# A decoder layer in one launch: first loads in smaller pieces from two queues, the first product by column halves, and r turned without copies

## The chip, the cores and the metric

The kernel runs on one core of one Trainium2 chip. The metric is the device time of one execution in microseconds (us), the median of three runs. The engines that matter are TensorE (PE, matrix products; PEld is its weight load), VectorE (DVE), ScalarE (ACT), GpSimd (POOL) and SyncE (SP, which here issues loads and stores). Each engine works through its own list of instructions strictly in that list's order and waits on semaphores where it needs the result of another engine or of a transfer. An instruction on SP or on ScalarE can also issue a transfer (DMA) between the chip's memory (HBM) and the on-chip buffers.

## The reference

One layer (DEPTH is 1) for a sequence of 1024 tokens with 1024 columns, all in 32-bit floats. What matters here:

```python
h = rms_norm(x, norm_mix_g)                 # r = (mean(x*x) + EPS) ** -0.5, a number per token
proj = h @ w_in                             # q, k, v, gates, convolution inputs ...
... gated linear attention, short convolution, merge, output projection ...
x = x + merged @ w_out
ple_gate = sigmoid(rms_norm(x, norm_ple_g) @ w_ple_gate)
x = x + ple_gate * (p @ w_ple_proj)         # p: 1024 x 256, w_ple_proj ("W_pe"): 256 x 1024
return rms_norm(x, norm_final_g)
```

The product `p @ w_ple_proj` depends on nothing else in the layer. The kernel computes it first, while x is still on its way, and keeps it in HBM until the end.

## The kernel before

*How a product is made.* Every 32-bit operand is split into a high part (a rounded copy, cast by ScalarE) and a low part (operand minus high part, by VectorE): `split`, line 594. A product is then three passes on TensorE, high by high, high by low and low by high (`mm3`, line 605). All passes accumulate in one PSUM bank of 128 rows by 512 columns.

*How the order comes about.* The kernel's code does not issue instructions, it notes them (`Flow.note`, line 270) with an estimated cost and latency each. `set_dues` gives every operation a due time, counted back from where TensorE's list of main products needs it. `put_in_order` then builds each engine's list greedily: at every step it takes the engine that can go first, and there, of the operations that are ready by the estimate, the one with the earliest due time. For a load issued by SP it models one shared pipe (`pipe`) for the landing. The field `hurry` moves due times forward. A changed estimate in the first microseconds can therefore change the order of later instructions too.

*The start* (phase `prep0`, from line 938). Nine products of zeros warm TensorE up. SP issues the loads of p (transposed on the host, as two contraction tiles of 128 rows each) and of W_pe (two tiles as well), each in pieces of 128 x 512, that is 256 KB: for the first half of p (`halves[0]`, tokens 0 to 511) and the first half of W_pe's columns first, W_pe and p in turn. The planner sets W_pe's piece first. After them come the second half of W_pe's columns, the x loads (`get_x`, tiles `hq`, 512 KB each), and the second half of p.

`pe_blocks` (line 1007) makes the product in blocks of 128 tokens by 512 columns. The first call takes tokens 0 to 511 (four blocks) and columns 0 to 511 with `by_kt=True`: all four blocks with the first contraction tile, then all four with the second. Each block and tile is one `mm3`, so the first call has 24 products, of which the first twelve need only the first tiles of p and W_pe. Finished blocks are copied out of PSUM by ScalarE and VectorE in turn and stored (`ped`).

*r of the input* (`scale_h`, line 976). ScalarE squares x (`sq`, `sr`), VectorE adds, TensorE sums over rows by products with a column of ones (`ms`), VectorE adds EPS and GpSimd takes the power -0.5 (`r_x`). r then stands with the token on the partition, and is wanted with the token along the columns and equal in all partitions: VectorE copies each of the four columns of r 128 times (`rb`, 128 x 512), TensorE transposes the four 128 x 128 squares (`rt`), and VectorE multiplies x by r and the gain (`hq`). `scale_h` runs twice, once for each half of the tokens.

*After the start* the layer's large products follow, first for the gates (`ga0pX` and so on), then the V stage (`vX`, `vV`, `vY`), into which the decay of the attention is woven: `zp` products, ScalarE's `t`, VectorE's `c` with a scan. From there on to the end TensorE works on products of the same form.

Of the kernel before, what the change touches and what calls it, by code (L numbers as in the profile page):

```python
# [16 lines left out]
P = 128  # L17
# [239 lines left out]
class Flow:  # L257
# [12 lines left out]
    def note(self, engine, op, call, args, kw):  # L270
        views = [a for a in args if isinstance(a, View) or hasattr(a, "ap")]
        views += [a for k, a in kw.items() if k not in ("out", "accum_out") and (isinstance(a, View) or hasattr(a, "ap"))]
        outs, ins = ([kw["out"]], views) if "out" in kw else (views[:1], views[1:])
        if kw.get("accum_out") is not None:
            outs.append(kw["accum_out"])
        o = Op()
        o.n, o.engine, o.call, o.args, o.kw = len(self.ops), engine, call, args, kw
        o.side, o.table, o.bytes, o.bufs, o.hurry = self.side, 0, 0, [], self.hurry
        label = lambda v: v.buf.name if isinstance(v, View) else "in"
        o.name = f"{label(outs[0])}<-{','.join(label(v) for v in ins)}"  # L280
        shape = outs[0].shape
        n = 1
        for d in shape[1:]:
            n *= d
        o.lat = 0.15
        if engine == PE:
            o.cost, o.lat = n / 2400 + 0.0134, 0.22
            if op == "transpose" or args[1].dtype == F32:
                o.cost = 0.11
            elif args[1].shape[0] < P:  # L290
                o.cost = 0.42
        elif engine == DVE:
            psum = any(isinstance(v, View) and v.buf.pool.name == "ps" for v in outs + ins)
            o.cost = 0.07 + n * (0.00055 if op in ("tensor_scalar", "tensor_copy") and not psum else 0.00104)
            if op in ("scalar_tensor_tensor", "tensor_scalar"):
                o.cost += 0.06
            if op == "tensor_tensor_scan":
                o.cost = 0.05 + n * 0.0021
        elif engine == ACT:
            o.cost = 0.10 + n * 0.000833 + (0.1 if "accum_out" in kw else 0.0)  # L300
            o.table = TABLE.get(args[2] if len(args) > 2 else None, 0)
        elif engine == POOL:
            o.cost = 0.1 + n * 0.001 if op == "memset" else 0.6
        else:
            o.cost, o.bytes = 0.4, shape[0] * n * 4
            if getattr(ins[0], "apart", None):
                o.cost, o.bytes = 0.6, 1.4 * o.bytes
            o.lat = 2.0 + o.bytes / 250e3
        preds = {}

        def behind(p):
            if p is not None and p != o.n:
                q = self.ops[p]
                lat = q.lat
                if q.engine == engine and engine != SP:
                    lat = 0.0 if engine == PE else 0.08
                preds[p] = max(preds.get(p, 0.0), lat)

        for v in ins:
            if isinstance(v, View):  # L320
                for b in v.blocks():
                    e = v.buf.memory.setdefault(b, [None, []])
                    behind(e[0])
                    e[1].append(o.n)
        for v in outs:
            if isinstance(v, View):
                for b in v.blocks():
                    e = v.buf.memory.setdefault(b, [None, []])
                    for p in [e[0]] + e[1]:
                        behind(p)  # L330
                    e[0], e[1] = o.n, []
                if engine == PE:
                    behind(v.buf.group)
                    v.buf.group = o.n
                for pool in v.buf.pool.instead:
                    for old in pool.buffers:
                        for p in old.users:
                            behind(p)
        for v in outs + ins:
            if isinstance(v, View) and v.buf not in o.bufs:  # L340
                if v.buf.index is None:
                    v.buf.index = len(v.buf.tag.buffers)
                    v.buf.tag.buffers.append(v.buf)
                o.bufs.append(v.buf)
                v.buf.users.append(o.n)
        o.preds, o.succs = preds, []
        for p in preds:
            self.ops[p].succs.append(o.n)
        self.ops.append(o)
        if self.bundle is not None and engine == PE:  # L350
            self.bundle.append(o)
# [163 lines left out]
def kernel(  # L515
# [83 lines left out]
    def mm(*a, **kw):  # L599
        nc.tensor.matmul(*a, skip_group_check=True, **kw)  # L600

    def transpose(o, i):
        nc.tensor.transpose(o, i, ident)
# [262 lines left out]
    def rows(b):  # L866
        return slice(b * P, (b + 1) * P)
# [70 lines left out]
    with phase("prep0") as pool:  # L938
# [10 lines left out]
        def get_x(i):  # L949
            for n in (0, 3) if i == 0 else (1, 2):  # L950
                for kp in range(0, 4, 2):
                    kk = 4 * quad[n][1] + kp
                    load(q[n][:, kp:kp + 2, :], xT[:, kk:kk + 2, halves[i]])

        nc.hurry = 8.0
        for kt in range(2):
            load(pr_[:, kt, halves[0]], pT[:, kt, halves[0]])
            load(wr_[:, kt, halves[0]], wpe[:, kt, halves[0]])
        for kt in range(2):
            load(wr_[:, kt, halves[1]], wpe[:, kt, halves[1]])  # L960
        nc.hurry = 0.0
        get_x(0)
        load(vec, vecs)
        for kt in range(2):
            load(pr_[:, kt, halves[1]], pT[:, kt, halves[1]])
        get_x(1)
        load(trim, tri)

        def split_half(hi, lo, src, hh):
            nc.hurry = 8.0  # L970
            for kt in range(2):
                cs = halves[hh]
                split(hi[:, kt, cs], lo[:, kt, cs], src[:, kt, cs])
            nc.hurry = 0.0

        def scale_h(i):


            both = (0, 3) if i == 0 else (1, 2)
            acc = slot(1, "hl"[i], f"sq{i}", (4, 512), F32)  # L980
            for j, (n, kp) in enumerate((n, kp) for n in both for kp in (0, 2)):
                d = acc[:, 0:2, :] if j == 0 else acc[:, 2:4, :] if j % 2 else slot(2, "hl"[i], f"sr{i}", (4, 512), F32)[:, 0:2, :]
                act(d, q[n][:, kp:kp + 2, :], AF.Square, scale=1.0 / 32.0)
                if j:
                    tt(acc[:, 0:2, :], acc[:, 0:2, :], d, op=ALU.add)
            sums = pso.tile([P, 4, P], F32, tag="o", name=f"ms{i}", bufs=2)
            for s in range(4):
                for kt in range(2):
                    mm(sums[:, s, 0:1], acc[:, kt, s * P:(s + 1) * P], ones, start=kt == 0, stop=kt == 1)
            r = sm.tile([P, 4], F32, tag="rx", name=f"r_x{i}", bufs=2)  # L990
            nc.vector.tensor_scalar(r, sums[:, :, 0], EPS, None, op0=ALU.add)
            nc.gpsimd.tensor_tensor(r, r, mhalf[:, 0:1].to_broadcast([P, 4]), op=ALU.pow)
            rb = bp.tile([P, 4, P], F32, tag="u2", name=f"rb{i}", bufs=2)
            nc.vector.tensor_copy(rb, r[:, :, None].to_broadcast([P, 4, P]))
            rt = pso.tile([P, 4, P], F32, tag="o", name=f"rt{i}", bufs=2)
            for s in range(4):
                transpose(rt[:, s, :], rb[:, s, :])
            rt = rt.rearrange("p s t -> p (s t)")
            for n in both:
                for k in range(4):  # L1000
                    kk = 4 * quad[n][1] + k
                    stt(q[n][:, k, :], q[n][:, k, :], gmix[:, kk:kk + 1], rt, op0=ALU.mult, op1=ALU.mult)
# [4 lines left out]
        def pe_blocks(bs, c, by_kt=False):  # L1007
# [5 lines left out]
            todo = [(b, kt) for kt in range(2) for b in bs] if by_kt else [(b, kt) for b in bs for kt in range(2)]  # L1013
            for b, kt in todo:
                nc.side = at[0] > len(BANKS)
                mm3(acc[b - bs[0]], pth[:, kt, rows(b)], ptl[:, kt, rows(b)], wph[:, kt, halves[c]],
                    wpl[:, kt, halves[c]], kt == 0, kt == 1)
                nc.side = True
                if kt == 1:
                    t = bp.tile([P, 512], F32, tag="T", name=f"pe{b}_{c}", bufs=4)  # L1020
                    (nc.vector.tensor_copy if b % 2 else nc.scalar.copy)(t, acc[b - bs[0]])
                    store(ped[b][:, halves[c]], t)
# [16 lines left out]
                c.cons(0, 0, X)  # L1039

        nc.hurry = 8.0
        for kt in range(2):
            split(pth[:, kt, halves[0]], ptl[:, kt, halves[0]], pr_[:, kt, halves[0]])
            split(wph[:, kt, halves[0]], wpl[:, kt, halves[0]], wr_[:, kt, halves[0]])
        nc.hurry = 0.0
        pe_blocks(range(0, 4), 0, True)
        split_half(wph, wpl, wr_, 1)
        pe_blocks(range(0, 4), 1)
        split_half(pth, ptl, pr_, 1)
        pe_blocks(range(4, 8), 0)  # L1050
        pe_blocks(range(4, 8), 1)
        scale_h(0)
# [747 lines left out]
```

## Time and profile before

| what | value |
|---|---|
| median of 3 runs | 1086.59 us (1086.43 to 1086.79) |
| the profiled execution, its own time | 1086.71 us |
| its span, first to last instruction | 1084.8 us |
| TensorE busy | 1071.5 us, 99% of the span |
| VectorE busy | 870.0 us, 80% |
| ScalarE busy | 598.9 us, 55% |
| GpSimd busy | 49.3 us, 5% |
| transfers | 237.85 MB, 219 GB/s in the mean |
| granted TensorE clock | 0.997 |

The span leaves out some 1.9 us of the execution that lie around it. Times in the profile's rows count from the span's start. A row of the timeline has the start, the length, the engine, the source line, the operation and "out <- in" by the program's tile names; nearly all operations carry line 503, where the planned order is issued, so they are told apart by tile names. In brackets stands how long the engine was idle before it and what it waited for. "SPq" is the issue of a transfer by SP, not the transfer itself. Products on TensorE overlap: the distance between two starts is the pace, and it is shorter than the length of one.

### The profile page before, as it was taken

Reading aid. Unit: us, or ns where it says so; the run is one execution under the profiler, and the core shown is the slowest. Engines: PE = TensorE matmul, PEld = TensorE weight load, DVE = VectorE, ACT = ScalarE, POOL = GpSimd, SP = SyncE. Lnnn points to the kernel's source line nnn. Section 1 sums busy time; section 2 is a strip of 40 time slices with the busy share of each in tenths; the row PEclk is TensorE's granted clock in tenths of the full one; section 3 lists DMA queues with packets and bytes.
Section 4 is the critical chain, followed back from the end, with each engine's and each line's share of the span. In section 5 each row is a group of like instructions: output and inputs, shape, how many; then the busy total and the mean of one; then the engine's idle time right before and its main releaser. Section 6 shows DMA issues by size and latency. Waiting matters only on the chain.

```text
span 1084.8 us, 14656 instructions
## 1 busy us (share of the span) xinstructions
PE 1071.5 (99%) x4893; PEld 890.8 (82%) x4893; DVE 870.0 (80%) x1343; ACT 598.9 (55%) x1071; POOL 49.3 (5%) x89
## 2 busy tenths in 40 slices
PE   9999999999999999999999999999999999999996
PEld 7887887888888888888888888888888888888885
DVE  6998567588997977856757788887999888889886
ACT  6777547657453455433333367766756635467554
POOL 0000000000000000000000012110000000012013
PEclk9999999999999999999999999999999999999998
DMA  8943554547776598231222679989586878799954
GB/s 306 342 164 117 175 181 163 161 168 241 216 228 216 193 313 279 68 107 49 69 87 68 227 253 334 327 296 331 197 306 210 288 223 304 242 336 327 312 191 155
DMA packets 144252, 237.85 MB, mean 219 GB/s; under 512 B 11953, under 2 KB 57265, under 8 KB 141233
## 3 DMA queue, kind: packets, MB, share of 16 engines
q1 hardware_dynamic: 144176, 236.93, 64.8%
q8 instruction: 38, 0.62, 0.3%
q14 instruction: 38, 0.30, 0.1%
HBM read 156.14 MB, written 80.74 MB: 218 GB/s over the span
## 4 chain that ended last, share of the span: by engine, by line
PE 96%; DVE 1%; ACT 1%; issue 1%; POOL 0%; DMA 0%; POOLq 0%; DVEq 0%; ACTq 0%
PE vY L503 3%; PE zaY L503 3%; PE pe L503 2%; PE zaV L503 2%; PE op L503 2%; PE vV L503 2%; PE zaX L503 2%; PE kv L503 1%; PE vX L503 1%; PE ga2Y L503 1%; PE ga0Y L503 1%; PE ga1Y L503 1%; PE ga3Y L503 1%; PE gc1Y L503 1%; PE cb3Y L503 1%; PE gc0Y L503 1%
## 5 line engine op out<-in xcount | busy, mean ns | idle before, releaser
L503 ACT ACTIVATE junk<-x 128x512 bf16<-128x512 f32 (+1 forms) x29 | 17.9, 616 | 19.0 <-DVE x L503 16.1
L503 ACT ACT_TABLE_LOAD x17 | 21.8, 1283 | 3.4 <-issue 2.4
L503 DVE TENSOR_TENSOR wt<-wt 128x512 f32<-128x512 f32 x32 | 21.6, 687 | 0.3
L503 POOL MEMSET t<- 128x2 f32 x8 | 0.8, 100 | 444.5 <-DMA qkd<-kk 245.6
L503 DVE SCALAR_TENSOR_TENSOR u<-t,vec,u 128x1024 f32<-128x1024 f32 x16 | 20.4, 1278 | 0.0
L503 POOL TENSOR_SCALAR rg<-ms 128x1 f32<-128x1 f32 x8 | 6.6, 823 | 261.2 <-ACT junk L503 261.0
L503 ACT ACTIVATE og<-op,or 128x256 f32<-128x256 f32 x32 | 13.3, 469 | 1.7 <-POOL or L503 1.7
L503 ACT CAST S<-S 128x512 fp32r<-128x512 f32 x14 | 8.7, 619 | 9.5 <-PE op L503 9.1
L503 ACT ACTIVATE oq<-oq,vec 128x512 f32<-128x512 f32 x20 | 13.3, 716 | 0.0
L503 ACT ACTIVATE junk<-op 128x256 bf16<-128x256 f32 x32 | 12.2, 380 | 1.7 <-PE op L503 1.4
L503 PE MATMUL pe<-wpehi,pThi 128*128 128x512 f32 x32 | 12.8, 400 | 0.0
L503 POOL TENSOR_TENSOR or<-or,mhalf 128x2 f32<-128x2 f32 x16 | 12.7, 795 | 1.3
L503 PE MATMUL pe<-wpehi,pTlo 128*128 128x512 f32 x32 | 12.7, 398 | 0.0
L503 PE MATMUL op<-v,aTh 128*128 128x256 f32 x64 | 12.6, 280 | 0.0
L503 PE MATMUL pe<-wpelo,pThi 128*128 128x512 f32 x32 | 12.6, 394 | 0.0
L503 DVE TENSOR_TENSOR szl<-og,szl 128x512 f32<-128x512 f32 x16 | 11.0, 686 | 1.7 <-ACT og L503 1.7
L503 DVE SCALAR_TENSOR_TENSOR S<-S,dds,kv 128x256 f32<-128x256 f32 x24 | 10.4, 474 | 1.8 <-PE kv L503 1.7
L503 DVE SCALAR_TENSOR_TENSOR hq<-hq,vec,rt 128x512 f32<-128x512 f32 x16 | 11.0, 744 | 1.0 <-PE rt L503 1.0
L503 DVE STREAM_TRANSPOSE oT<-szl 128x512 f32<-128x512 f32 x16 | 11.3, 705 | 0.2
L503 DVE TENSOR_TENSOR u<-u,s 128x512 f32<-128x512 f32 x16 | 10.9, 689 | 0.3
L503 DVE TENSOR_TENSOR x<-x,pe 128x512 f32<-128x512 f32 (+1 forms) x17 | 11.0, 655 | 0.2
L503 DVE SCALAR_TENSOR_TENSOR x<-x,rf,gfin 128x1024 f32<-128x1024 f32 (+2 forms) x8 | 8.9, 1113 | 2.7 <-POOL rf L503 2.7
(2905 smaller groups left out, 4106.3 us busy)
## 6 DMA issues: line engine op xcount, KB each, us to landing
wtd<-wt SPq DMA_DIRECT2D x44, 256.0 KB, 3.9
wt<-in_wb_dram SPq DMA_DIRECT2D x8, 1024.0 KB, 7.2
v<-vd SPq DMA_DIRECT2D x16, 512.0 KB, 5.3
wgq<-wtd SPq DMA_DIRECT2D x7, 1024.0 KB, 7.0
qk<-qkd SPq DMA_DIRECT2D x12, 512.0 KB, 5.5
vraw<-in_wv_dram SPq DMA_DIRECT2D x20, 256.0 KB, 3.6
zaraw<-in_wv_dram SPq DMA_DIRECT2D x20, 256.0 KB, 4.0
uq<-ud SPq DMA_DIRECT2D x5, 1024.0 KB, 9.1
```

The source lines that it names most:

```text
L503: o.call(*[place(a) for a in o.args], **{k: place(a) for k, a in o.kw.items()})
```

## The change

Three things change.

1. The first loads. p's first tile is loaded as its first 128 tokens (`near`) and the other 384 of the half (`far`), W_pe's first tile as two column halves of 256 (`left`, `right`). `near`, `right` and the 512 columns of W_pe's second tile are issued by ScalarE, the others by SP. The second half of p is loaded in two transfers, of 128 and of 384 tokens, each for both contraction tiles. The splits follow the same pieces. The planner gets an estimate for transfers that SP doesn't issue: cost 0.4 and latency 2.3 us plus bytes over 250 per nanosecond, without the shared pipe.
2. The first product of the first block (high by high) is made in two column halves of 256, the rest of it as before.
3. The copies `rb` are gone: the transpose reads a column of r as a 128 x 128 square with a step of zero.

```diff
@@ Flow.note
+        if op == "dma_start" and engine != SP:
+            o.cost, o.lat = 0.4, 2.3 + shape[0] * n * 4 / 250e3
@@ prep0, loads
+        near, far, left, right = slice(0, P), slice(P, 512), slice(0, 256), slice(256, 512)
         nc.hurry = 8.0
-        for kt in range(2):
-            load(pr_[:, kt, halves[0]], pT[:, kt, halves[0]])
-            load(wr_[:, kt, halves[0]], wpe[:, kt, halves[0]])
+        nc.scalar.dma_start(pr_[:, 0, near], pT[:, 0, near])
+        load(wr_[:, 0, left], wpe[:, 0, left])
+        nc.scalar.dma_start(wr_[:, 0, right], wpe[:, 0, right])
+        load(pr_[:, 0, far], pT[:, 0, far])
+        nc.scalar.dma_start(wr_[:, 1, halves[0]], wpe[:, 1, halves[0]])
+        load(pr_[:, 1, halves[0]], pT[:, 1, halves[0]])
         for kt in range(2):
             load(wr_[:, kt, halves[1]], wpe[:, kt, halves[1]])
         nc.hurry = 0.0
         get_x(0)
         load(vec, vecs)
-        for kt in range(2):
-            load(pr_[:, kt, halves[1]], pT[:, kt, halves[1]])
+        for cs in (slice(512, 640), slice(640, SEQ)):
+            load(pr_[:, :, cs], pT[:, :, cs])
...
@@ scale_h
-            rb = bp.tile([P, 4, P], F32, tag="u2", name=f"rb{i}", bufs=2)
-            nc.vector.tensor_copy(rb, r[:, :, None].to_broadcast([P, 4, P]))
             rt = pso.tile([P, 4, P], F32, tag="o", name=f"rt{i}", bufs=2)
             for s in range(4):
-                transpose(rt[:, s, :], rb[:, s, :])
+                transpose(rt[:, s, :], r[:, s:s + 1].to_broadcast([P, P]))
@@ pe_blocks
-                mm3(acc[b - bs[0]], pth[:, kt, rows(b)], ptl[:, kt, rows(b)], wph[:, kt, halves[c]],
-                    wpl[:, kt, halves[c]], kt == 0, kt == 1)
+                ph_, pl_, o = pth[:, kt, rows(b)], ptl[:, kt, rows(b)], acc[b - bs[0]]
+                if by_kt and b == kt == 0:
+                    mm(o[:, left], ph_, wph[:, 0, left], start=True, stop=False)
+                    mm(o[:, right], ph_, wph[:, 0, right], start=False, stop=False)
+                    mm(o, ph_, wpl[:, 0, halves[0]], start=False, stop=False)
+                    mm(o, pl_, wph[:, 0, halves[0]], start=False, stop=False)
+                else:
+                    mm3(o, ph_, pl_, wph[:, kt, halves[c]], wpl[:, kt, halves[c]], kt == 0, kt == 1)
@@ prep0, splits
-        for kt in range(2):
-            split(pth[:, kt, halves[0]], ptl[:, kt, halves[0]], pr_[:, kt, halves[0]])
-            split(wph[:, kt, halves[0]], wpl[:, kt, halves[0]], wr_[:, kt, halves[0]])
+        for hi, lo, src, kt, cs in ((pth, ptl, pr_, 0, near), (wph, wpl, wr_, 0, left), (wph, wpl, wr_, 0, right),
+                                    (pth, ptl, pr_, 0, far), (wph, wpl, wr_, 1, halves[0]), (pth, ptl, pr_, 1, halves[0])):
+            split(hi[:, kt, cs], lo[:, kt, cs], src[:, kt, cs])
         nc.hurry = 0.0
         pe_blocks(range(0, 4), 0, True)
-        split_half(wph, wpl, wr_, 1)
+        split_part(wph, wpl, wr_, halves[1])
         pe_blocks(range(0, 4), 1)
-        split_half(pth, ptl, pr_, 1)
+        split_part(pth, ptl, pr_, slice(512, 640))
+        split_part(pth, ptl, pr_, slice(640, SEQ))
```

`split_part` does for a range of columns what `split_half` did for a half. In the lists that the planner builds for the changed kernel, ScalarE's begins with the issues of `right`, `near` and W_pe's second tile, then its table load, then the casts of `right`, `near`, W_pe's second tile, `left`, `far`, p's second tile, and the two of W_pe's second column half. SP's begins with `left`, `far`, p's second tile, W_pe's second column half in two pieces, and the first x loads. The lists of all engines differ from those of before up to the V stage and are the same from there on.

More of the change, by code (lines that the diff above doesn't have):

```diff
@@ L963, with split_part @@
         load(vec, vecs)
-        for kt in range(2):
-            load(pr_[:, kt, halves[1]], pT[:, kt, halves[1]])
+        for cs in (slice(512, 640), slice(640, SEQ)):
+            load(pr_[:, :, cs], pT[:, :, cs])
         get_x(1)
         load(trim, tri)
-        def split_half(hi, lo, src, hh):
+        def split_part(hi, lo, src, cs):
             nc.hurry = 8.0
             for kt in range(2):
-                cs = halves[hh]
                 split(hi[:, kt, cs], lo[:, kt, cs], src[:, kt, cs])
```

## The prediction

> **What bounds the kernel now.** I read the page's totals first, then its chain of work that ended last, then that chain's first 60 us, and last the timeline of the first 10 us.
>
> ```profile
> span 1084.8 us, 14656 instructions
> PE 1071.5 (99%) x4893; PEld 890.8 (82%) x4893; DVE 870.0 (80%) x1343; ACT 598.9 (55%) x1071; POOL 49.3 (5%) x89
> PE 96%; DVE 1%; ACT 1%; issue 1%; POOL 0%; DMA 0%; POOLq 0%; DVEq 0%; ACTq 0%
> ```
>
> TensorE is busy for 99% of the span and is 96% of the chain: after the start, nearly every product follows the one before it. What the change can move is when that stream begins, what holes its first products have, and one later hole, priced below.
>
> ```profile
> 1.44 4.21 PE warm L503 x9
> 5.64 13.75 PE pe L503 x57
> 19.40 1.68 PE ms L503 x16
> ```
>
> The stream is nine warm-up products, then `pe` (p times W_pe), then `ms` (the sums for r). The timeline shows what the first `pe` products wait for. Columns: start, length, engine, what; in brackets the idle time before and its releaser.
>
> ```profile
> 0.72 1.28 ACT L503 ACT_TABLE_LOAD   x1 [0.72 <-PEq L1789]
> 0.72 0.38 SPq L503 DMA_DIRECT2D wperaw<-in_wpe_dram  x1
> 1.16 0.42 SPq L503 DMA_DIRECT2D pTraw<-in_pT_dram  x1
> 1.63 0.43 SPq L503 DMA_DIRECT2D wperaw<-in_wpe_dram  x1
> 2.10 0.43 SPq L503 DMA_DIRECT2D pTraw<-in_pT_dram  x1
> 3.52 0.43 SPq L503 DMA_DIRECT2D hq<-in_xT_dram  x1
> 3.96 0.62 ACT L503 CAST wpehi<-wperaw 128x512 fp32r<-128x512 f32 x1 [1.96 <-DMA wperaw<-in_wpe_dram]
> 4.67 0.62 ACT L503 CAST pThi<-pTraw 128x512 fp32r<-128x512 f32 x1
> 5.44 0.50 PE L503 MATMUL pe<-wpehi,pThi 128*128 128x512 f32 x1
> 6.37 0.62 ACT L503 CAST wpehi<-wperaw 128x512 fp32r<-128x512 f32 x1 [1.07 <-DMA wperaw<-in_wpe_dram]
> 6.41 0.39 PE L503 MATMUL pe<-wpehi,pThi 128*128 128x512 f32 x1
> 7.95 0.62 ACT L503 CAST pThi<-pTraw 128x512 fp32r<-128x512 f32 x1 [0.96 <-DMA pTraw<-in_pT_dram]
> 8.26 0.40 PE L503 MATMUL pe<-wpehi,pTlo 128*128 128x512 f32 x1
> 9.35 0.19 PEld L503 LDWEIGHTS pe<-wpehi,pTlo 128*128 128x128 f32 x1 [0.43 <-DVE pTlo L503]
> 9.69 0.39 PE L503 MATMUL pe<-wpehi,pThi 128*128 128x512 f32 x1
> ```
>
> Four 256 KB pieces land at 3.96, by 4.67, at 6.37 and at 7.95 (where ScalarE's waits end). The first product starts at 5.44, where the warm-up ends, so the start has no idle time worth a microsecond. Numbering the `pe` products from 0, number 3 starts at 6.41, 11 at 8.26 (a pace of 0.23 us) and 15 at 9.69; from there the stream does not stop. Without any hole number 15 would start at 5.44 + 15 x 0.23 = 8.89, so **the most that a better start can win is 0.8 us**.
>
> **The change, part by part.** *Loads.* Of the six loads of the first half of p and of the first half of W_pe, the first row block, three are issued by ScalarE (W_pe right 128 KB, p near 64 KB, W_pe of the second contraction tile 256 KB, "W1" below) and three by SP (W_pe left 128 KB, p far 192 KB, p of the second tile 256 KB, "p1"). Bytes are the same. ScalarE's three issues at 0.38 to 0.43 us push its table load from 0.72 to about 2.1; with 1.28 us it ends at 3.4, still ahead of the first landing at 3.96, so this costs nothing; without that cover it would be up to 1.3 us.
>
> *The order on ScalarE.* This is the step that counts. The changed program has ScalarE cast in the order right, near, **W1, left**, far, p1. The planner's figure for a ScalarE load is its own (2.3 us plus bytes), so it puts the cast of W1 ahead of that of left. ScalarE works in order, so left, far and p1 queue behind the landing of the 256 KB of W1, and TensorE's very first product (left columns) waits for the left cast; VectorE's second subtraction waits for it too. The trace of before shows no load from ScalarE, so W1's landing is bounded. It is issued third on its queue, at about 1.63. Served alone, 448 KB of its own queue land between the first 256 KB (3.96) and 512 KB (4.67): 4.5. With both queues served equally 896 KB have gone by: halfway between the third piece of before (6.37) and the fourth (7.95), 7.2; as late as the fourth, 7.95. I take 6.37, the row it is nearest to: a 256 KB piece of W_pe, issued third at 1.63.
>
> ```profile
> 4.00:5.00 1.00, 1.00 (x3) 0.73 (x3) 0.40 (x1) 0.90 (x2) 0.00 (x0) 1.00 0.91 277
> 7.00:8.00 1.00, 1.00 (x6) 0.82 (x5) 0.69 (x1) 0.05 (x1) 0.00 (x0) 1.00 0.93 320
> 27.22 0.62 ACT L503 CAST ga0phi<-ga0praw 128x512 fp32r<-128x512 f32 x1
> 27.74 1.05 ACT L503 CAST h0hi<-hq 128x1024 fp32r<-128x1024 f32 x1
> 23.75 0.68 DVE L503 TENSOR_TENSOR ga2plo<-ga2praw,ga2phi 128x512 fp32r<-128x512 f32 x1
> 27.58 1.22 DVE L503 TENSOR_TENSOR h0lo<-hq,h0hi 128x1024 fp32r<-128x1024 f32 x1
> ```
>
> In the two windows of the first block the last columns are the DMA engines' busy share and GB/s: 0.91 and 0.93 with SP's queue alone, so a second queue finds little idle capacity. The Trainium skill ("DMA: Bandwidth & Descriptors", section "Issuing engines are not separate DMA queues") says that loads issued by SP and by ScalarE run on the same 16 engines and interleave, so a second issuer saves issue time alone; those shares agree, and by that rule the equal-service figure of 7.2 would hold and the sum below would be +2.1 in place of +1.35.
>
> The last rows price the pieces: a cast of 512 columns takes 0.62 us and lets the next start 0.52 later, 1024 take 1.05; so 256, 128 and 384 columns take 0.41, 0.30 and 0.51. On VectorE 0.68 and 1.22 give 0.41, 0.28 and 0.55.
>
> The sum: W1's cast starts at 6.37, left's at 6.89 and ends at 7.30; the first product follows 0.15 later, as in before (4.67 + 0.62 to 5.44): **7.45 in place of 5.44**. Left's low part runs on VectorE 7.35 to 7.76, near's 7.67 to 7.95, far's (its cast 7.20 to 7.71) 7.86 to 8.41. So products 1 to 5 start at about 7.82, 8.05, 8.28, 8.51 and 8.74. Product 15 follows ten paces later, at 11.04, without the later holes: p1 lands at 7.95 at the latest seen, is cast by 8.6, and W1's and p1's low parts end at 9.0 and 9.6, before product 14 at 10.8. Against 9.69 this is **+1.35 us**. The formula is landing of W1 minus 5.02.
>
> *Column halves.* Four instructions for three, with the same columns in all: 0; one weight load more (0.19 in its row above) runs beside the products. Ends: 0 and +0.2.
>
> *Smaller pieces elsewhere.* The second half of p comes as 128 and 384 columns: two casts and two subtractions more. With the two that the first pieces add, ScalarE has 0.8 us more. In the window 9.69 to 19.24 it is busy for 7.60 of 9.55, and these pieces are wanted only after 33 more products. SP's first x load waits for the first ScalarE load's semaphore (about 4.0 in place of 3.52); the DMA engines have a backlog then, so 0. Ends: 0 and +0.3.
>
> ```profile
> 9.69:19.24 9.55, 9.55 (x44) 7.88 (x43) 7.62 (x10) 7.60 (x11) 0.00 (x0) 1.00 1.04 394
> L503 DVE COPY rb<-r_x x2: 426/426/427, 22.8 to 45.4; 128x512 f32<-128x512 f32 x2
> PEld rt L503 <- DVE rb L503: 0.2, 1, 0.2
> PE vV L503 <- DVE c L503: 1.2, 1, 1.2
> ```
>
> *r without copies.* Two VectorE copies of 0.43 go. TensorE waited 0.2 us for one; but the planner now sets the turn one product (0.23) earlier after `ms`, so that wait may stay, for GpSimd's power instead. I take 0; ends -0.2 and +0.2. The weight load reads one column 128 times over; its row of before reads a written-out copy, so a slower read is unseen: with eight of them at 0.14 us, doubling is +1.1 at worst, and I take 0 because it reads no more elements.
>
> *Planner's knock-on.* The four decay products `zp` and some casts of the V stage change places; after that all queues have the same order. TensorE waits there 1.2 us for VectorE's `c`. In both programs five VectorE instructions stand between the scans and that `c`: 0, with ends -1.2 and +1.2.
>
> The profiled execution took 1086.71 us, 0.12 above the median of 1086.59. 1086.71 + 1.35 = **1088.1**.
>
> **The rivals.** *W1 later still* (the fourth piece's 7.95): +2.9, 1089.6. For it: small pieces on both queues alternate, and the late pieces of before kept landing late. Against: fewer bytes are ahead of W1 than of the fourth piece. It passes 0.2% when W1 lands after 7.1.
>
> *The change does what it says, and the kernel is faster.* Place: W1's landing. If ScalarE's queue is served early, W1 is there at 4.5 and the first product starts at 5.57; p1, after 576 KB of its own queue, would be there at 4.67 + 0.25 x 1.70 = 5.1 and no hole is left: product 15 at 5.57 + 1.29 + 2.3 = 9.16, **-0.5 us, 1086.2**; if p1 still lands at 7.95 it is about 0, 1086.7. It decides if W1 lands before 5.02. For it: there are two queues. Against: the busy shares of 0.91 and 0.93.
>
> *The array slows while it waits.* The nine warm-up products started 0.44 us apart (1.44 to 5.44), later ones 0.23. TensorE would now stand idle for some 2 us after them. If that sends it back to the early pace for as long as at the start, nine products at 0.21 us more cost 1.9: +3.25, 1090.0. The holes of before, 0.43 at most in the rows above, did not. The Trainium skill ("TensorE: Matmul & The Clock Gate", Part 1) puts the half-rate state after an idle window of about 3.4 us, longer than the 2 us expected here; no row of before shows such a wait.
>
> *The V stage.* The hole of 1.2 us closes or doubles: 1086.9 or 1089.3.
>
> **How the numbers follow.** The chances: forecast 0.52 (W1 between 5.4 and 7.2, thus its own range 1087.1 to 1088.9), W1 later 0.16, faster or level 0.15, slow array 0.12, V stage 0.05. I hold 0.2%, 2.2 us or 1084.4 to 1088.8, for about what a measurement of this kernel tells from no change. Above it lie nearly all of "later" and of "slow array" and a little of the forecast and of the V stage: 0.31. Below it lies only an early W1 together with a closed hole: 0.02. The rest, 0.67, is within. The range 1086.0 to 1090.1 leaves out part of the two ends, some 0.15.
>
> **What would show it.** In the changed profile: ScalarE's casts as right, near, W1, left, with the idle time ahead of W1's cast put down to a DMA; the first `pe` product near 7.5, released by ScalarE's cast; number 15 near 11.0; no waits in the `pe` products after that; no copies of r; the V stage's wait near 1.2. I am wrong if W1's cast starts before 5.4 or after 7.2, if products keep a pace of 0.4 us after 7.5, or if the V stage's hole moves.

## The result and the profile after

The changed kernel takes 1090.16 us in the median of 9 runs (1088.31 to 1091.25); the kernel before, run beside it, 1086.79 us (9 runs, 1086.43 to 1087.03). The ratio is 1.003, 95% interval 1.0022 to 1.0038: slower, by 3.4 us. The forecast was 1088.1 in a range of 1086.0 to 1090.1, with most of the chance on a change within 0.2%; the median lies 0.06 us above that range, and the change is beyond 0.2%. The profiled execution of the changed kernel is its slowest run, 1091.25 us with a span of 1089.1, against 1086.71 and 1084.8 before: +4.5 in time, +4.3 in span. What follows explains those 4.3; the median run has about a microsecond less.

The page's totals and its chain that ended last, for the changed kernel:

```profile
span 1089.1 us, 14664 instructions
PE 1073.6 (99%) x4894; PEld 892.9 (82%) x4894; DVE 868.5 (80%) x1345; ACT 598.4 (55%) x1075; POOL 49.3 (5%) x89
PE 95%; DVE 2%; ACT 1%; DMA 1%; issue 1%; POOL 0%; POOLq 0%; ACTq 0%; DVEq 0%
```

TensorE is still the bound, and its busy time rose by 2.1 us with practically the same products: products take longer somewhere. The chain up to 30 us says where it begins (start, length, what):

```profile
1.64 5.94 DMA wperaw<-in_wpe_dram
7.60 0.93 ACT wpehi L505 x2
8.58 15.22 PE pe L505 x56
23.80 1.68 PE ms L505 x16
```

Before, the chain began with the warm-up products on TensorE. Now it begins with one load, W1, issued by ScalarE at 1.64, and its cast. The timeline shows the rest (start, length, engine, what; in brackets the idle time before and its releaser):

```profile
1.44 4.21 PE L505 MATMUL warm<-zero 128*128 128x512 f32 x9 [1.44 <-DVE zero L505]
2.12 1.28 ACT L505 ACT_TABLE_LOAD   x1 [2.12 <-issue]
4.24 0.41 ACT L505 CAST wpehi<-wperaw 128x256 fp32r<-128x256 f32 x1 [0.84 <-DMA wperaw<-in_wpe_dram]
5.06 0.30 ACT L505 CAST pThi<-pTraw 128x128 fp32r<-128x128 f32 x1 [0.41 <-DMA pTraw<-in_pT_dram]
7.60 0.92 ACT L505 CAST wpehi<-wperaw 128x512 fp32r<-128x512 f32 x2 [2.24 <-DMA wperaw<-in_wpe_dram]
8.58 0.80 PE L505 MATMUL pe<-wpehi,pThi 128*128 128x256 f32 x2 [2.93 <-ACT wpehi L505]
10.06 0.63 PE L505 MATMUL pe<-wpehi,pThi 128*128 128x512 f32 x1
10.48 0.63 PE L505 MATMUL pe<-wpelo,pThi 128*128 128x512 f32 x1
13.47 0.54 PE L505 MATMUL pe<-wpehi,pTlo 128*128 128x512 f32 x1
13.85 0.39 PE L505 MATMUL pe<-wpehi,pThi 128*128 128x512 f32 x1
14.08 0.40 PE L505 MATMUL pe<-wpelo,pThi 128*128 128x512 f32 x1
14.55 0.39 PE L505 MATMUL pe<-wpehi,pThi 128*128 128x512 f32 x1
```

ScalarE casts right, near, then stands idle for 2.24 us until W1 lands, and casts W1 and left in one row of two. TensorE, idle for 2.93 us, starts at 8.58 in place of 5.44. And it starts slowly: two neighbours at 10.06 and 10.48 are 0.42 us apart and 0.63 long, up to 13.47; from 13.85 they are 0.23 apart and 0.39 long. The slow pace is that of the warm-up, whose nine products took 4.21 us. Product 15 (the two halves count as product 0) starts at 14.55 against 9.69, **+4.86**. With the fast pace throughout it would have been at 7.60 + 4.67 = 12.27 by the prediction's formula, so the late load is 2.58 of it and the slow pace 2.28.

The other place where the programs differ is the V stage. TensorE's longer waits in the changed kernel, and the first and last starts of two groups of products, of before and of after:

```profile
PE pe L505 <- ACT wpehi L505: 2.9, 1, 2.9
PE vV L505 <- DVE c L505: 0.5, 1, 0.5
```

```profile
L503 PE MATMUL vX<-v0hi,h0hi x16: 387/389/395, 76.2 to 90.5; 128*128 128x512 f32 x16
L503 PE MATMUL zaV<-za1hi,h1hi x16: 389/389/389, 186.8 to 197.0; 128*128 128x512 f32 x16
```

```profile
L505 PE MATMUL vX<-v0hi,h0hi x16: 387/389/395, 81.1 to 95.4; 128*128 128x512 f32 x16
L505 PE MATMUL zaV<-za1hi,h1hi x16: 389/389/389, 191.2 to 201.4; 128*128 128x512 f32 x16
```

The V stage's wait for `c` fell from 1.2 to 0.5 us. (The expectations below give this hole as the distance between the two starts less one pace, 1.4 and 0.7.) `vX` begins 4.9 us later than before and `zaV` 4.4 later: of the 0.7 gained at the wait, 0.5 remains. From there the shift stays the same to the end: 4.86 - 0.5 is the 4.3 of the span.

### The profile page after: what moved, and what is told of

The parts are those of the page before. It is cut to its first block, busy times and chain, and to the rows that moved or that the text cites. A ratio compares the mean times of both kernels' runs of the same rounds, so it can differ in the third digit from the quotient of the medians.

```text
span 1089.1 us, 14664 instructions
## 1 busy us (share of the span) xinstructions
PE 1073.6 (99%) x4894; PEld 892.9 (82%) x4894; DVE 868.5 (80%) x1345; ACT 598.4 (55%) x1075; POOL 49.3 (5%) x89
## 4 chain that ended last, share of the span: by engine, by line
PE 95%; DVE 2%; ACT 1%; DMA 1%; issue 1%; POOL 0%; POOLq 0%; ACTq 0%; DVEq 0%
PE vY L505 3%; PE zaY L505 3%; PE pe L505 2%; PE zaV L505 2%; PE op L505 2%; PE vV L505 2%; PE zaX L505 2%; PE kv L505 1%; PE ga2Y L505 1%; PE ga0Y L505 1%; PE ga1Y L505 1%; PE ga3Y L505 1%; PE gc1Y L505 1%; PE cb3Y L505 1%; PE gc0Y L505 1%; PE gt1Y L505 1%
## 5 line engine op out<-in xcount | busy, mean ns | idle before, releaser
L505 PE MATMUL pe<-wpehi,pThi 128*128 128x512 f32 (+1 forms) x33 | 13.6, 418 | 2.9 <-ACT wpehi L505 2.9
L505 PEld LDWEIGHTS pe<-wpehi,pThi 128*128 128x128 f32 x33 | 6.9, 213 | 5.1 <-ACT wpehi L505 3.7
```

Of the source, the lines that this page charges most:

```text
L505: o.call(*[place(a) for a in o.args], **{k: place(a) for k, a in o.kw.items()})
```

## The experiments

The theory: ScalarE's cast of W1, placed ahead of left's, makes the first product wait for W1's landing; that wait and the slow pace after it are the whole loss. The main rivals: the second queue or the small pieces cost something by themselves; the turn of r costs something; the array is slow whether it waits or not. All ratios are against runs of the kernel before on the same chip.

**Only the cast's place.** In the changed kernel's finished order, W1's cast is moved behind far's:

```diff
+        casts = [o for o in order if o.engine == ACT and o.name in ("wpehi<-wperaw", "pThi<-pTraw")]
+        w1, far = casts[2], casts[4]
+        order.remove(w1)
+        order.insert(order.index(far) + 1, w1)
```

> The changed kernel with one instruction moved on ScalarE: the cast of W1 (W_pe's second tile) goes behind the casts of left and far; loads, queues and all other engines' orders stay. Theory (the order on ScalarE is the cost): near lands at about 5.0, so the first product starts near 5.8 in place of 8.58, its number 15 near 9.9 in place of 14.55 at the full pace, and the kernel takes 1086.2 to 1087.0 us (before: 1086.8), with a small spread. Rival (the second queue itself makes the loads late, whatever the order): the first product stays past 7 us and the kernel past 1088.5.

Measured: 1086.3 us (1085.5 to 1086.61, 11 runs) against 1086.76, ratio 0.9994, interval 0.9985 to 1.0003. The timeline of this kernel:

```profile
5.09 0.40 ACT L509 CAST wpehi<-wperaw 128x256 fp32r<-128x256 f32 x1
5.40 0.51 ACT L509 CAST pThi<-pTraw 128x384 fp32r<-128x384 f32 x1
6.82 0.62 ACT L509 CAST wpehi<-wperaw 128x512 fp32r<-128x512 f32 x1 [0.91 <-DMA wperaw<-in_wpe_dram]
5.55 0.80 PE L509 MATMUL pe<-wpehi,pThi 128*128 128x256 f32 x2
6.60 0.63 PE L509 MATMUL pe<-wpehi,pTlo 128*128 128x512 f32 x1
7.44 0.40 PE L509 MATMUL pe<-wpelo,pThi 128*128 128x512 f32 x1
9.98 0.39 PE L509 MATMUL pe<-wpehi,pThi 128*128 128x512 f32 x1
```

Moving one cast takes away the whole loss of 3.4 us. ScalarE still waits for W1, 0.91 us, but nothing that TensorE needs early is queued behind it. The first products are slow here too, until 7.4, without any wait before them: product 15 is at 9.98, still 0.29 later than before, and the V stage gives back 0.5. Two queues, small pieces, halves and the new turn of r together cost nothing that can be measured.

**Only the order, in the kernel before.** One queue, whole pieces, copies of r: only W1's cast is moved ahead of the first cast of W_pe.

```diff
+        casts = [o for o in order if o.engine == ACT and o.name == "wpehi<-wperaw"][:2]
+        order.remove(casts[1])
+        order.insert(order.index(casts[0]), casts[1])
```

> The kernel before with one instruction moved on ScalarE: the cast of W1 goes ahead of the cast of W_pe's first tile. One queue, large pieces, copies of r, all as before. Theory (order alone is enough): W1 lands at 6.4 as in before, the first product starts near 8.2 in place of 5.44, number 15 between 11.8 (full pace) and 14.4 (0.43), the kernel 1088.9 to 1091.5 with a spread of some 2 us. Rival (it takes the second queue): at most 1087.5.

Measured: 1089.79 us (1087.37 to 1090.78, 6 runs) against 1086.76, ratio 1.0025, interval 1.0014 to 1.0036. So the order alone, without any of the change's other parts, makes nearly the whole loss. W1 landed early here, at 5.64, and the first product started at 7.36, but product 15 only at 12.84, +3.15. The timeline of TensorE, and the windows of the same kernel (length; TensorE's busy time and count; granted clock; DMA share; GB/s):

```profile
7.36 0.50 PE L506 MATMUL pe<-wpehi,pThi 128*128 128x512 f32 x1 [1.86 <-ACT pThi L506]
7.69 0.39 PE L506 MATMUL pe<-wpelo,pThi 128*128 128x512 f32 x1
8.83 0.63 PE L506 MATMUL pe<-wpelo,pThi 128*128 128x512 f32 x1
11.39 0.63 PE L506 MATMUL pe<-wpelo,pThi 128*128 128x512 f32 x1
12.14 0.39 PE L506 MATMUL pe<-wpehi,pThi 128*128 128x512 f32 x1
12.84 0.40 PE L506 MATMUL pe<-wpehi,pThi 128*128 128x512 f32 x1
```

```profile
5.20:8.60 3.40, 1.45 (x6) 1.00 0.97 287
8.60:12.00 3.40, 3.40 (x10) 0.50 1.01 353
```

The product at 7.69 is fast (0.39), those from 8.83 to 11.39 are slow (0.63), and the clock column says 0.50 for just that stretch. The array was at full pace when the warm-up ended, waited for 1.86 us, and fell back afterwards. At the fast pace product 15 would have followed at 7.36 + 3.45 = 10.81 at the earliest, so the slow pace is up to 2.0 of the 3.15. (The clock column holds only from the first clock record on: it says 1.00 in the changed kernel up to 13.8 as well, where the lengths of 0.63 show the slow pace.)

**The planner's estimate.** The rule in `Flow.note` behind the order: an operation that follows one of its own engine gets 0.08 us of latency. That is meant for computation, but a transfer that ScalarE issued and a cast on ScalarE also have one engine, so the cast counts as ready 0.08 us after the issue, and the new figure of 2.3 us plus bytes is not used for it. The edit in the changed kernel:

```diff
-                if q.engine == engine and engine != SP:
+                if q.engine == engine and engine != SP and q.lat < 1.0:
```

> The changed kernel with one condition in the planner: the short latency of 0.08 us that it gives to a predecessor on the same engine no longer holds for a load that ScalarE issues. The planner then orders the casts left, right, near, far, p1, W1, and may move instructions of later stages as well. Theory: as with the moved cast alone, a first product near 5.8 and 1086.0 to 1087.2, the V stage's hole being free to move by 1.2 either way. Rival (second queue): past 1088.5.

Measured: 1086.12 us (1085.73 to 1087.68, 11 runs) against 1086.76, ratio 0.9996, interval 0.9987 to 1.0005. ScalarE's casts now come as left, right, near, far, p1, W1; the first product starts at 5.75 and product 15 at 9.51, 0.18 earlier than before. The planner's new order also brought a hole of 1.1 us after 169.4 (`zp` among the `zaX` products). The misjudged latency is the origin of the order.

**A longer warm-up.** In the changed kernel 23 warm-up products in place of 9, so that TensorE does not stand idle before the first product:

```diff
-    for n in range(9):
+    for n in range(23):
```

> The changed kernel with 23 warm-up products in place of 9, which reach to about 8.4 us; nothing else. Theory (late start and slow array are two costs): the first product still starts near 8.6, but the pace after it is 0.23 us at once; number 15 near 12.2 in place of 14.55, the kernel near 1088.3 (1087.8 to 1088.8), and the runs spread by less than 1 us in place of 2.9. Rival (the pace of 0.43 comes from the operands or the transfers): the pace and 1090.2 stay.

Measured: 1088.83 us (1088.23 to 1089.61, 11 runs) against 1086.76, ratio 1.0019, interval 1.001 to 1.0028. TensorE's timeline:

```profile
4.59 5.07 PE L505 MATMUL warm<-zero 128*128 128x512 f32 x16
9.50 0.40 PE L505 MATMUL pe<-wpehi,pThi 128*128 128x256 f32 x2
9.73 0.40 PE L505 MATMUL pe<-wpelo,pThi 128*128 128x512 f32 x1
12.93 0.39 PE L505 MATMUL pe<-wpehi,pThi 128*128 128x512 f32 x1
```

W1's cast started at 7.61, as in the profile of the changed kernel. The warm-up ran on to 9.5, too long by 0.9 us, so that the first product starts later than in the changed kernel; yet product 15 is at 12.93 against 14.55, because every product has the fast pace. 1.3 us of the median's 3.4 come back; 0.9 more would by the same rows if the warm-up ended with W1's cast. This separates the two terms: the late load and, beside it, the slow pace. The median lies just above the expected range. The spread shrinks, from 2.9 to 1.4 us, but not below the 1 us expected.

**One queue.** The changed kernel with all six first loads issued by SP:

```diff
-        nc.scalar.dma_start(pr_[:, 0, near], pT[:, 0, near])
+        load(pr_[:, 0, near], pT[:, 0, near])
...
```

> The changed kernel with all first loads issued by SP, in the same small pieces; product in column halves, r without copies. The planner's casts then follow the loads: left, right, far, near, W1, p1. Theory (pieces and second queue are worth nothing in themselves, the order costs): the four pieces of the first tiles, 512 KB, are there by 4.7 as in before, the first product starts near 5.7, number 15 near 9.7, and the kernel takes 1086.0 to 1087.2 us. Rival (smaller pieces are slow, or the second queue helps): beyond 1087.5.

Measured: 1087.04 us (1086.25 to 1088.72, 10 runs) against 1086.92, ratio 1.0005, interval 0.9995 to 1.0014. The planner now knows the landings, and the order is that of need. W1 still landed at 7.00, and p1 at 8.74 made a hole of its own (ScalarE, then TensorE):

```profile
7.00 0.62 ACT L505 CAST wpehi<-wperaw 128x512 fp32r<-128x512 f32 x1 [1.53 <-DMA wperaw<-in_wpe_dram]
8.74 0.62 ACT L505 CAST pThi<-pTraw 128x512 fp32r<-128x512 f32 x1 [1.12 <-DMA pTraw<-in_pT_dram]
9.41 0.50 PE L505 MATMUL pe<-wpehi,pThi 128*128 128x512 f32 x1 [0.73 <-ACT pThi L505]
```

The first product is at 5.52 and product 15 at 10.47, +0.78 in this execution and later than the 9.7 expected. Pieces, halves and r in another form of the kernel again make no difference that the runs can tell. The V stage's wait is 1.2 here, as before.

**r alone.** The kernel before without the copies `rb`, the order of everything else kept. The copies are dropped from the finished order, and the transposes are given r's columns, read with a step of zero (`self.columns`, noted in `scale_h`):

```diff
+        order = [o for o in order if not o.name.startswith("rb")]
+        for o in order:
+            if o.name.startswith("rt") and "rb" in o.name:
+                o.args = (o.args[0], self.columns[o.args[1].buf.name][o.args[0].off // P], o.args[2])
```

> The kernel before with the two copies of r left out and the transposes reading r's columns with a step of zero; every engine's order is otherwise that of before. Theory: the weight loads of the transposes stay at 0.14 us, the copies' 0.85 us on VectorE were covered, the V stage's hole stays at 1.4: 1086.8, within 0.4 us of before. Rival (the repeated read is slow): 0.5 to 1.1 us more.

Measured: 1086.8 us (1086.1 to 1087.79, 10 runs) against 1086.92, ratio 1.0003, interval 0.9993 to 1.0012. The weight loads that turn r, before and in this kernel (min, median and max in ns):

```profile
L503 PEld LDWEIGHTS rt<-ident,rb x8: 138/139/146, 23.3 to 46.9; 128*128 128x128 f32 x8
```

```profile
L508 PEld LDWEIGHTS rt<-ident,r_x x8: 134/136/137, 23.2 to 47.1; 128*128 128x128 f32 x8
```

Reading one column 128 times over costs no more than reading a written-out copy. The V stage's wait stayed at 1.2.

**The copies put back.** The changed kernel with `rb` again, all else as changed:

```diff
+            rb = bp.tile([P, 4, P], F32, tag="u2", name=f"rb{i}", bufs=2)
+            nc.vector.tensor_copy(rb, r[:, :, None].to_broadcast([P, 4, P]))
...
-                transpose(rt[:, s, :], r[:, s:s + 1].to_broadcast([P, P]))
+                transpose(rt[:, s, :], rb[:, s, :])
```

> The changed kernel with the copies of r put back, planned anew. Theory (r's part is worth nothing at the start): W1's cast still stands ahead of left's, the first product starts past 7.5 us, and the kernel takes 1089 to 1091, as the changed one. What the V stage's hole does tells which part of the change moved it: 0.7 if it was the loads, 1.4 if it was r's copies.

Measured: 1091.73 us (1091.1 to 1091.91, 4 runs) against 1086.92, ratio 1.005, interval 1.0033 to 1.0067, so 4.8 us above the kernel before, where the changed kernel was 3.4 above, and 0.7 above the expected range. With four runs, and intervals that overlap, the difference of 1.4 is not certain; the returned V stage wait of 1.2 in place of 0.5 would explain a part. W1's cast started at 6.80, the first product at 7.78, and the slow pace lasted until 11.4. Here too the clock had been full and fell back: its windows say 1.00 from 4.8 to 8.2 with TensorE busy for 0.93 of 3.40 us, then 0.50 to 11.6. The wait for `c` needs both parts to become shorter: it is 0.5 with two queues and no copies (the changed kernel, the moved cast, the mended planner rule and the version with both gains, below), but 1.2 with either part alone; with the longer warm-up the wait lies elsewhere, at a `vX` product (0.6). In the kernels with the short wait the fourth `zp` stands three products earlier among TensorE's. This points to the planner's order rather than to r or the loads as such: dropping r's copies in an unchanged order left the wait at 1.2. The loads were not tested in an unchanged order.

**A second look at the changed kernel**, unaltered.

> The changed kernel once more, for a second look at the same program. Theory: W1 is cast between 6.4 and 8 us, the first product follows 1.0 us later, and the array reaches its full pace at another time than 13.8, since its clock steps do not start with the program; the time follows both. Rival (late landing and slow pace belong to that one execution): a first product before 6.5.

Measured: 1091.1 us, span 1088.9. W1's cast started still later, at 8.18, after 2.82 us of waiting; the first product at 9.16, product 15 at 14.86. The slow pace ended in both executions at 13.8. The expectation thus missed twice: the cast came after its range of 6.4 to 8, and the full pace did not come at another time. The late landing and the slow pace did come back, so they do not belong to one execution.

**A version with both gains.** From the changed kernel, ScalarE's first six casts as left, right, near, far, p1, W1, all other lists kept:

```diff
+        casts = [o for o in order if o.engine == ACT and o.name in ("wpehi<-wperaw", "pThi<-pTraw")]
+        where = sorted(order.index(o) for o in casts[:6])
+        right, near, w1, left, far, p1 = casts[:6]
+        for at, o in zip(where, (left, right, near, far, p1, w1)):
+            order[at] = o
```

> The changed kernel with one thing altered: ScalarE's first six casts are put as left, right, near, far, p1, W1 into the places that they had; the lists of all other engines stay those of the changed kernel. Both gains seen so far should then stand in one kernel: the start as with the planner's delay for ScalarE's own loads (first product 5.75, product 15 at 9.51, against 9.69 in the kernel before, -0.18 us) and the shorter hole in the V stage (0.68 against 1.37, -0.69), without the hole of 1.1 us further on that the planner's own new order brought. The theory that the start and the V stage's hole add up expects a span of 1084.8 - 0.18 - 0.69 = 1083.9 and a median some 0.8 us under that of the kernel before, about 1086.0, ratio 0.9992, at the edge of what 5 rounds tell from 1. The rival, that the array's pace at the start decides more than the order, expects product 15 anywhere between 9.3 and 11 and a median within 0.5 us of the kernel before.

Measured: 1086.47 us (1085.91 to 1087.17, 11 runs) against 1086.29, ratio 1.0002, interval 0.9993 to 1.0011. The gain of 0.8 us that the theory expected (ratio 0.9992) did not show. The profiled execution has a span of 1083.8, close to the expected 1083.9, with product 15 at 9.63 and a V stage wait of 0.5; but it was the fastest of its eleven runs, its products were only 0.5 us ahead of those of before, and the rest of its gain came after the last product. No version was measurably faster than the kernel before.

## Why the prediction was right in the place and short in the size

The prediction's sum was +1.35 us and its range ended at 1090.1; the median is +3.4, the profiled execution +4.5. All three signs that it named for being wrong came: W1's cast after 7.2 (7.60), a pace of 0.4 us after 7.5 (0.42), and a V stage hole that moved (1.2 to 0.5). That the median still lies at the range's edge is partly luck: the range reached to either rival alone (1089.6 and 1090.0), both came together, and the V stage took 0.5 back.

- *The order on ScalarE* came as forecast: right, near, W1, left, with the wait ahead of W1's cast put down to its load. That it is the loss is shown by moving this one cast away (0.9994) and, nearly in full, by moving it alone in the kernel before (1.0025).
- *The reason given for that order was wrong.* The prediction said that the planner uses the new figure of 2.3 us plus bytes for ScalarE's loads. It uses 0.08 us, since load and cast are on one engine; the edit of that rule put W1's cast last.
- *W1's landing* was the mis-sized term: 6.37 was taken, between bounds of 4.5 and 7.95; it measured 7.60 and 8.18 in two executions of the changed kernel, and 7.61, 6.82 and 6.80 in three others with that load on ScalarE's queue. In two more, where no cast waited for it (the planner's rule, both gains), it landed 5.0 and 5.3 us after its issue at 1.64, at 6.6 and 6.9. Issued by SP it landed at 6.37, 5.64, 5.35 and 7.00. The formula held: landing + 1.08 gives a first product at 8.68, measured 8.58. The row that was taken, 6.37, came from a queue that had the engines to itself; that this is why it was too early was not shown. The sentence from the Trainium skill ("DMA: Bandwidth & Descriptors", section "Issuing engines are not separate DMA queues") that loads of two issuers interleave on the same engines, by which the prediction put 7.2, agrees better: the seven landings on ScalarE's queue average 7.2, though they range from 6.6 to 8.2.
- *The array slows while it waits* was held apart as a rival with +1.9 more; the slow pace came together with the late load. But in the changed kernel the array did not slow down: its first clock record is the full step at 13.78, so it was still at the warm-up's pace, and the wait kept it there. A fall from the full pace was seen in the kernel with only the order changed and in that with the copies back. From 8.58 to 13.85 twelve products took 5.27 us; at the forecast's pace they take 1.29 + 7 x 0.23 = 2.90. That is 2.37, less the 0.1 by which the first product came ahead of the formula: 2.28 to within rounding. The mistake was to price the two as alternatives, although both hang on the same wait.
- *The V stage* was set at 0 with ends of 1.2 either way: 0.7 less wait, 0.5 less in the end. The count of five VectorE instructions between the scans and `c` said nothing on when TensorE would arrive there.
- *Column halves, smaller pieces, r without copies, the table load*: nothing measurable, as forecast. The table load ended at 3.40, ahead of the first landing. r alone measured 1.0003, the pieces and halves with one queue 1.0005, all together in the right order 0.9994.
- *The run's own terms:* of product 15's +4.86 in the profile, 1.35 was forecast, 1.23 is W1's later landing (7.60 for 6.37) and 2.28 the pace.

## What to carry to other kernels

Work that an in-order engine must do on a late load should stand behind all that is wanted earlier: one cast in the wrong place cost 3.4 us, and all the loads' other forms nothing that could be measured. When a planner or a list decides the order, look at what latency it gives a transfer whose issuer and user are the same engine. Price a wait of TensorE near the start with the slow pace that can follow it (here about 2 us beside a wait of 2 to 3), and not as the wait alone.

## What the runs showed of the hardware

*The clock moves in steps of 3.41 us, and part-time work does not hold it.* In the kernel before with only the order changed, the trace's clock records say full at 5.19, half at 8.60, full at 12.01; with the copies back 4.78, 8.19, 11.60. In the stretches before the fall TensorE was busy for 1.45 and 0.93 of 3.40 us, idle for no more than 2.5 at a time. In both executions of the changed kernel the first full step came at 13.78, although the nine warm-up products had run for 4.2 us. Counted back from that step, the stretches of 3.41 us hold 2.10, 2.11, 1.79 and 3.41 us of work in the profile above: the warm-up lay across two of them and filled neither, and the wait emptied part of the third. In six executions without the long wait the first full step came between 4.4 and 7.5 (the kernel before 5.57, the version with both gains 4.37, r alone 7.48). The Trainium skill ("TensorE: Matmul & The Clock Gate", Part 1, "What's actually happening") describes a free-running window of 3413 ns that decides on the clock; the steps agree. Its table there puts the half rate after an idle window; here a stretch with 1.45 us of work was enough to fall back.

The starts of all eleven profiles agree with a decision at the end of each such stretch by its busy share. The full step came after 2.93 us of work in 3.41 (86%, both gains) and not yet after 2.63 (77%, r alone) or 2.56 (75%, the moved cast). The full pace was held after 2.96 us (87%, one queue) and lost after 1.45 (43%). The share was not varied by itself, and the stretches ahead of the first record are counted back, not recorded; where the limits lie between these figures stays open.

*The same bytes land at different times.* W1, 256 KB issued third on its queue, landed between 6.6 and 8.2 in seven executions. Together with the clock's steps, whose place against the program's start differs from run to run, this may be why the changed kernel spreads over 2.9 us; the longer warm-up, which removes the clock's part, spread over 1.4. Neither cause was separated in the spread, and the kernel before, 0.6 in the nine runs beside the changed kernel, spread over 1.5 to 2.6 in the larger sets beside the experiments. What holds back single landings was not settled.

*The end of the span varies too.* After the last product, equal programs ended some tenths of a microsecond apart. In the second execution of the changed kernel the last product started 0.25 us later than in the first, yet the span was 0.2 shorter. In the version with both gains, whose lists are those of before once the V stage is past, the products were 0.5 us earlier than before and the span 1.0 shorter. A difference below half a microsecond between two single profiles is therefore no effect by itself.
